# A decoder block on one core: gate and up products of the FFN summed on PSUM banks that ScalarE fills, in another order of the seven

## The chip, the core and the metric

The kernel runs on one core of one Trainium2 chip. A core has a matmul engine (TensorE; PE in the profile, PEld its weight loads), three engines for elementwise work (VectorE: DVE, ScalarE: ACT, GpSimd: POOL), a queue that mostly issues transfers (SyncE: SP), an on-chip memory (SBUF) and a small accumulator memory for matmul results (PSUM, eight banks). Each engine takes its instructions in the order of the program and waits at each for the semaphores that it names.

The metric is the device time of one execution in microseconds.

## The reference

The block normalises x (512 tokens, 2048 channels), runs two kinds of attention side by side, projects their outputs, and then runs a SwiGLU feed-forward layer with a hidden width of 5632, all in float32:

```python
def reference(x, norm1_g, w_in, ..., w_gate, w_up, w_down, final_g):
    ...
        hn = rmsnorm(h, norm1_g[l])
        proj = hn @ w_in[l]
...
        h = h + mixed @ w_out[l]

        hn2 = rmsnorm(h, norm2_g[l])
        h = h + (jax.nn.silu(hn2 @ w_gate[l]) * (hn2 @ w_up[l])) @ w_down[l]
    return rmsnorm(h, final_g)
```

Nearly all of the change lies in `hn2 @ w_gate` and `hn2 @ w_up`.

## The kernel before

**Split operands.** Every float32 operand of a large matmul is split in two: a high part (ScalarE copies it to fp32r) and a low part (VectorE subtracts the high part from the source). A product is then three matmuls: high·high, high·low and low·high (`mm`, lines 1037 to 1040, in the FFN; `mm3`, lines 167 to 169, elsewhere). The weights arrive from memory as `raw` tiles of 128 x 1024, two halves of 512 columns each. A `Job` (line 123) splits one half: `first()` runs an optional `prep`, then ScalarE writes `wh` (line 136); `second()` has VectorE write `wl` (line 139) and then runs an optional `post`. There are five slots of `wh` and five of `wl`, and four of `raw` (`LA = 4`). `next_half()` (line 174) gives PE the next split half; before that it issues the splits up to three halves ahead, the `second()` of a job one step behind its `first()`. It also issues what `later(n, f)` has put off: `f` is issued n halves after the present one, behind the splits of that step, and in the order in which it was put off. So each engine's order is written by this program order, and a waiting instruction holds all behind it on its engine.

**The FFN.** The hidden width is cut into 44 blocks f of 128. Per block, gate and up are computed together as a 2 x 2 block product by seven half-size products instead of eight (a Strassen-Winograd form). The tokens are cut into a low and a high half of 256 (`LO`, `HI`), the 2048 input channels into two halves. The four weight quarters A11, A21, A22, A12 of a block are the four `raw` tiles of that block; VectorE adds one to another in place (`comb`, line 778) to form the sums that the seven products need. Each combination is for one half of 512 columns, so there are eight per block. The activations' seven operands (B11, T1, T2, T3, T4, B21, B22) are made once, ahead of the FFN (`terms`, lines 950 to 1005).

A product (`product`, line 1025) is two halves of 12 matmuls of 128 x 256, summed in one PSUM bank. P1, P7, P4, P6 and P5 have a bank each; from block 1 on P2 goes on in the bank of P1, and P3 in the bank of P5. `after(f, name)` (line 1055) takes the results out: after P1 ScalarE copies P1 to `g` (line 1070), after P6 VectorE makes two sums with P6 and P7, after P5 two with P5 and P4, after P2 the low half of g times the factor `r2` of the second norm, after P3 the sum for g's high half (line 1087) and its product with `r2` (line 1088). Each of these is put off by one half with `later(1, ...)`. `finish` (line 1042) then does silu(g) on ScalarE (line 1045), u·g on VectorE (line 1048), its high part `ah` on ScalarE (line 1049) and its low part `al` on VectorE (line 1053), in steps that are put off by further halves, so they fall into the next block.

After every fourth block its four hidden blocks are multiplied by `w_down`: the 16 output rows of that down-projection (`down`, line 1091; a half of 24 matmuls each, weights in `rawd` tiles) are mixed into the next block's list, four behind each product from the third on. Blocks without them are called plain blocks in what follows. Block 0 has an order of its own, `ORDER0`, and forms part of its weight sums by adding transfers.

The order of the seven, and the products' jobs with their combinations, stand in `quad_jobs` (lines 770 to 823); the loads of the next block's tiles are issued by the `post` of P6, P5 and P3.

**Other places that the change touches.** `Spread` (line 232) turns four columns of factors into a row for all partitions: VectorE scales an identity matrix four times (line 239), PE multiplies it with ones. `compressed` (line 399) is the small network over compressed keys and values. The first transfers of the program are those of `sm` (all gains; line 280) and of x and the first weights, all on SP.

Of the kernel before, what the change touches and what calls it, by code (L numbers as in the profile page):

```python
# [71 lines left out]
def block_kernel(ctx: ExitStack, tc: tile.TileContext, xt, wst, wdn, smalls, wg, w2c, bias, ident_in, out):  # L72
# [25 lines left out]
    raws = {}  # L98
    state = {"dma": 0, "split": 0}
    LA = 4  # L100

    def load_to(n):
        while state["dma"] < min(n, len(units)):
            u = state["dma"]
            t = wp.tile([128, 1024], F32, tag="raw", name="raw", bufs=LA)
            for k in range(2 if u < TWO else 1):
                c = slice(512 * k, 512 * k + 512) if u < TWO else slice(0, 1024)
                sp.dma_start(t[:, c], wst[u][:, c])
            raws[u] = t
            state["dma"] += 1  # L110
            if units[u] == ("quad", 0, 1):
                pool_e.dma_start(t, wst[u + 1], accum_op=OP.add)
# [119 lines left out]
    class Spread:  # L232


        def __init__(self, col):
            self.n = col.shape[-1]
            self.r = base.tile([128, 512], F32, tag="r", name="r", bufs=2)
            for t in range(self.n):
                dve.tensor_scalar(self.r[:, 128 * t:128 * t + 128], ident, col[:, t:t + 1], None, op0=OP.mult)

        def __call__(self, copy=True, tag="misc", bufs=1):
            pb = ps.tile([128, 512], F32, tag=tag, name="prb", bufs=bufs)
# [34 lines left out]
    def tmp(name="tmp"):  # L277
        return ap_.tile([128, S], F32, tag="tmp", name=name, bufs=3)

    sp.dma_start(sm, smalls)  # L280
    xc = {}

    def load_x(k):
# [115 lines left out]
    def compressed(s):  # L399
        pt = ps.tile([128, 512], F32, tag="misc", name="phidt")  # L400
        for hb in range(2):
            for i in range(2):
                pe.matmul(pt[:, 64 * hb:64 * hb + 64], hids[:, s, 128 * hb:128 * hb + 128],
                          ident[:, 64 * i:64 * i + 64], start=(i == 0), stop=(i == 1))
        h = hidt[s]
        for hb in range(2):
            c = slice(64 * hb, 64 * hb + 64)
            if s == 0:
                act.activation(h[:, hb, 0, :], pt[:, c], AF.Silu)
            else:  # L410
                for g in range(2):
                    c = slice(64 * hb + 32 * g, 64 * hb + 32 * g + 32)
                    act.activation(h[:, hb, g, :, :], pt[:, None, c].to_broadcast([128, 3, 32]), AF.Silu)
        yield
        p2 = ps.tile([128, 512], F32, tag="misc", name="pcmp")
        if s == 0:
            for hb in range(2):
                pe.matmul(p2[:, :64], w2[:, hb, :], h[:, hb, 0, :], start=(hb == 0), stop=(hb == 1))
            dve.tensor_copy(kc, p2[:, :64])
        else:  # L420
            for g in range(2):
                for hb in range(2):
                    pe.matmul(p2[:96, 128 * g:128 * g + 128], h[:, hb, g, :, :],
                              w2[:, 2 + hb, :], start=(hb == 0), stop=(hb == 1))
                v = et_h[:, 7 + 3 * g, :]
                act.activation(v[:96], p2[:96, 128 * g:128 * g + 128], AF.Copy)
                dve.tensor_tensor(v[32:64], p2[32:64, 128 * g:128 * g + 128], v[32:64].bitcast(F32), op=OP.subtract)
# [336 lines left out]
    def load_fin(n):  # L764
        while len(fin) < min(n, KB // 2):
            k = 2 * len(fin)
            fin.append(wp.tile([128, 1024], F32, tag="raw", name="fin", bufs=LA))
            sp.dma_start(fin[-1].rearrange("p (n c) -> p n c", n=2), wdn[NPH - 1, k:k + 2].rearrange("n p c -> p n c"))

    def quad_jobs(f, order):  # L770

        u = base_u + 4 * f

        def q(i, k):
            return raws[u + i][:, 512 * k:512 * k + 512]

        def comb(o, x):
            return lambda: dve.tensor_tensor(o(), o(), x(), op=OP.add)  # L778

        def fetch(o, i, k):  # L780

            return lambda: pool_e.dma_start(o(), wst[u + i][:, 512 * k:512 * k + 512], accum_op=OP.add)

        def nxt(i):
            return lambda: load_to(u + 4 + i + 1)

        r = {}
        for k in range(2):
            A11, A21, A22, A12 = (lambda i=i, k=k: q(i, k) for i in range(4))

            if f == 0:
                r["P1", k] = Job(A11, load=None if k else nxt(-1), post=fetch(A11, 1, k))
                r["P5", k] = Job(A21, post=fetch(A21, 0, k))
                r["P7", k] = Job(A11)
                r["P2", k] = Job(A12)
                r["P4", k] = Job(A22, prep=comb(A12, A21))
                r["P6", k] = Job(A21)
                r["P3", k] = Job(A12)
            else:
                r["P1", k] = Job(A11)  # L800
                r["P7", k] = Job(A11, prep=comb(A11, A21))
                r["P4", k] = Job(A22, post=comb(A21, A22))
                r["P5", k] = Job(A21)
                r["P6", k] = Job(A22, prep=comb(A22, A11))
                r["P2", k] = Job(A12)
                r["P3", k] = Job(A12, prep=comb(A12, A22))
        if f + 1 < FB:
            if f == 0:
                r["P6", 1].post = nxt(2)
                r["P3", 1].post = nxt(3)  # L810
            else:
                r["P6", 1].post = nxt(0)
                r["P5", 1].post = nxt(1)
                r["P3", 1].post = nxt(3)
        else:
            r["P6", 1].post = lambda: load_fin(1)
            r["P5", 1].post = lambda: load_fin(2)
            r["P3", 1].post = lambda: load_fin(LA)
        r["P1", 0].even = f in (1, 2) or f % 8 == 5
        return [r[p, k] for p in order for k in range(2)]  # L820

    ORDER0 = ("P1", "P5", "P2", "P7", "P4", "P6", "P3")
    ORDER = ("P1", "P7", "P4", "P6", "P5", "P2", "P3")

    def dn_job(p, nb):
        return Job(lambda: dn[p, nb], post=load_dn)
# [123 lines left out]
    def terms(nb):  # L950
# [41 lines left out]
        def s3():  # L992
            dve.scalar_tensor_tensor(t[:, HI], k[:, LO], gk, t[:, LO], op0=OP.mult, op1=OP.add)
            low("T3", n, t[:, LO])
            high("T2", n, t[:, HI])

        def s4():
            dve.scalar_tensor_tensor(t[:, LO], h[:, LO], g, t[:, HI], op0=OP.mult, op1=OP.subtract)
            low("T2", n, t[:, HI])
            high("T4", n, t[:, LO])  # L1000

        def s5():
# [16 lines left out]
             for n, t in (("P1", "proj"), ("P7", "proj"), ("P4", "sc"), ("P6", "sc"), ("P3", "t"))}  # L1019
    banks["P5"] = ps.tile([128, 512], F32, tag="o", name="P5")  # L1020
    dbanks = {}

    st = {}

    def product(f, name):
        key = {"P2": "P1", "P3": "P5" if f else "P3"}.get(name, name)
        if key == name:
            st[key] = banks[name]
        p = st[key][:, :256]
# [1 line left out]
        for k in range(2):  # L1031
            h, l = next_half()
            for s in range(4):
                mm(p, h[:, 128 * s:128 * s + 128], l[:, 128 * s:128 * s + 128], th[:, 4 * k + s, :],
                   tl[:, 4 * k + s, :], key == name and k == 0 and s == 0, k == 1 and s == 3)

    def mm(o, wh, wl, mh, ml, start, stop):
        pe.matmul(o, wh, mh, start=start, stop=False, skip_group_check=True)  # L1038
# [16 lines left out]
    def after(f, name):  # L1055
# [10 lines left out]
        g, u = st.get("g"), st.get("u")  # L1066
        if name == "P1":
            st["g"] = ft()
            st["u"] = ft() if f else None
            act.activation(st["g"][:, LO], x("P1"), AF.Copy)  # L1070
        elif name == "P6":
            sub(g[:, HI], g[:, LO], x("P6"))
            add(u[:, LO], g[:, HI], x("P7"))
            if not f:
                dve.tensor_tensor(g[:, LO], x("P1"), st["r2"][:, LO], op=OP.mult)
                add(u[:, HI], u[:, LO], x("P5"))
                sub(u[:, LO], u[:, LO], x("P4"))
                add(g[:, HI], g[:, HI], x("P5"))
        elif name == "P5":
            add(u[:, HI], u[:, LO], x("P5"))  # L1080
            sub(u[:, LO], u[:, LO], x("P4"))
        elif name == "P2":
            dve.tensor_tensor(g[:, LO], x("P1"), st["r2"][:, LO], op=OP.mult)
            if f == FB - 1:
                finish(f, g, u, LO)
        elif name == "P3":
            add(g[:, HI], g[:, HI], x("P5" if f else "P3"))
            dve.tensor_tensor(g[:, HI], g[:, HI], st["r2"][:, HI], op=OP.mult)
            finish(f, g, u, HI if f == FB - 1 else slice(0, 512))

# [19 lines left out]
    for kind, a, b in sched:  # L1110
# [5 lines left out]
        if f == 0:  # L1116
            if name == "P7":
                r = st["rs2"] = Rsqrt(tokens(sacc), D, rab.v[:, :4])
                r.invert()
                dve.tensor_tensor(r.z, r.z, rab.y[:, :4], op=OP.mult)  # L1120
                later(1, lambda r=r: st.update(inv=Spread(r.z), r2=Spread(r.y)))
            if name == "P6":
                st["inv"] = st["inv"](False)
                act.activation(st["rs2"].rs[:, 7, :1], ones[:, :1], AF.Silu)
# [1 line left out]
                st["u"] = ft()  # L1126
            if name in ("P1", "P6", "P3"):
                later(0 if name == "P1" else 1, lambda name=name: after(0, name))
        elif name in ("P1", "P6", "P5", "P2", "P3"):
            later({(FB - 1, "P2"): 0, (FB - 1, "P3"): 3}.get((f, name), 1), lambda f=f, name=name: after(f, name))  # L1130

    def last():
# [7 lines left out]
        def scaled(r, nb, n, th):  # L1140
            h = hs[:, nb:nb + n, (LO, HI)[th]]
            o = h
            if th:
                if nb % 4 == 0:
                    st["o"] = wp.tile([128, 1024], F32, tag="raw", name="scaled", bufs=LA)
                o = st["o"].rearrange("p (a b) -> p a b", b=256)[:, nb % 4:nb % 4 + n, :]
            dve.tensor_tensor(o, h, r[:, None, :256].to_broadcast([128, n, 256]), op=OP.mult)
            sp.dma_start(out[th, :, nb:nb + n, :], o)
# [131 lines left out]
```

## Time and profile before

| | us |
|---|---|
| median of three runs | 2176.18 (2175.72 to 2179.32) |
| the profiled execution, its own time | 2175.39 |
| its span, first to last instruction | 2173.6 |
| granted PE clock, mean | 0.998 |

The profile is that of one execution. "Busy" is the time in which an engine had an instruction in work; matmuls overlap, so the mean duration of a matmul is longer than the distance from one to the next, and that distance is what a stretch costs. The same holds for VectorE and ScalarE: the next instruction can begin before the last has landed. In timelines the first two columns are the start and the duration in microseconds; a bracket at the end of a row gives the idle time of that engine ahead of the instruction and what ended it. In the list of waits the columns are the total waited, how often, and the longest; in lists of groups they are count, busy time, mean duration in ns, and idle time ahead.

The FFN begins at 836 us of the span and ends at about 2158, with the last sums and the output behind it.

### The profile page before, as it was taken

How to read it: one execution, taken by the hardware profiler on the slowest of the kernel's cores; microseconds unless marked ns; L12 is line 12 of the kernel's file. 1: busy time of each engine (PE TensorE's matmuls, PEld its weight loads, DVE VectorE, ACT ScalarE, POOL GpSimd, SP SyncE). 2: the span in 40 equal slices, each digit the busy share in tenths (PEclk: the TensorE clock that was granted, in tenths of full speed). 3: DMA queues.
4: the chain of work that ended last, by engine and by line, in shares of the span. 5: the costliest groups of instructions: out<-in, count | busy, mean ns of one | idle time of the engine just before them, and what ended most of it. 6: DMA issues, size and time to landing. Idle time of an engine off the chain costs nothing.

```text
span 2173.6 us, 39728 instructions
## 1 busy us (share of the span) xinstructions
PE 2159.9 (99%) x15776; PEld 2021.9 (93%) x15776; DVE 1566.0 (72%) x3046; ACT 965.9 (44%) x1862; POOL 42.7 (2%) x51
## 2 busy tenths in 40 slices
PE   9999999999999999999999999999999999999997
PEld 7888888888888889999999999999999999999997
DVE  6755565456667588979687777869596877878686
ACT  6544444344444255525343443435253434434356
POOL 0000000000000000000000000000000000000003
PEclk9999999999999999999999999999999999999999
DMA  6442222322224334333333333333333333333233
GB/s 224 150 135 80 90 77 70 102 80 81 80 78 164 98 97 101 115 116 100 108 105 117 97 109 106 108 96 108 117 98 107 108 117 92 114 107 108 81 124 107
DMA packets 81866, 232.28 MB, mean 107 GB/s; under 512 B 8848, under 2 KB 11536, under 8 KB 81680
## 3 DMA queue, kind: packets, MB, share of 16 engines
q1 hardware_dynamic: 80960, 228.17, 33.4%
q0 software_dynamic: 720, 1.57, 0.4%
q8 instruction: 124, 2.03, 0.4%
q14 instruction: 62, 0.51, 0.1%
HBM read 225.51 MB, written 4.19 MB: 106 GB/s over the span
## 4 chain that ended last, share of the span: by engine, by line
PE 98%; DVE 1%; ACT 0%; DMA 0%; issue 0%; SPq 0%; DVEq 0%; ACTq 0%
PE P L1040 15%; PE P L1038 15%; PE P L1039 15%; PE pp L167 7%; PE pp L169 7%; PE pp L168 7%; PE pd L1040 4%; PE pd L1039 4%; PE pd L1038 4%; PE pab L169 3%; PE pab L167 3%; PE pab L168 3%; PE pt L533 1%; PE po L168 1%; PE psc L169 1%; PE po L167 1%
## 5 line engine op out<-in xcount | busy, mean ns | idle before, releaser
L136 ACT ACTIVATE wh<-raw 128x512 fp32r<-128x512 f32 x888 | 548.7, 628 | 528.0 <-PE P L1039 208.7
L139 DVE TENSOR_TENSOR wl<-raw,wh 128x512 fp32r<-128x512 f32 x888 | 599.5, 687 | 43.9 <-ACT wh L136 42.5
L1040 PE MATMUL P<-ah,wl 128*128 128x256 f32 x1552 | 428.9, 276 | 0.2 <-DVE wl L139 0.2
L1038 PE MATMUL P<-ah,wh 128*128 128x256 f32 x1552 | 428.8, 276 | 0.0
L1039 PE MATMUL P<-al,wh 128*128 128x256 f32 x1552 | 428.8, 276 | 0.0
L1040 PEld LDWEIGHTS P<-ah,wl 128*128 128x128 f32 x1552 | 291.4, 188 | 0.4 <-DVE wl L139 0.4
L1039 PEld LDWEIGHTS P<-al,wh 128*128 128x128 f32 x1552 | 291.4, 188 | 0.0
L1038 PEld LDWEIGHTS P<-ah,wh 128*128 128x128 f32 x1552 | 291.4, 188 | 0.0
L167 PE MATMUL pp<-ah,wh 128*128 128x512 f32 x640 | 260.6, 407 | 0.0
L169 PE MATMUL pp<-ah,wl 128*128 128x512 f32 x640 | 251.1, 392 | 0.0
L168 PE MATMUL pp<-al,wh 128*128 128x512 f32 x640 | 250.3, 391 | 0.0
L778 DVE TENSOR_TENSOR raw<-raw 128x512 f32<-128x512 f32 x346 | 237.7, 687 | 3.4
L1040 PE MATMUL pd<-ah,wl 128*128 128x256 f32 x784 | 216.6, 276 | 0.0
L1039 PE MATMUL pd<-al,wh 128*128 128x256 f32 x784 | 216.5, 276 | 0.0
L1038 PE MATMUL pd<-ah,wh 128*128 128x256 f32 x784 | 216.5, 276 | 0.0
L136 ACT ACTIVATE wh<-rawd 128x512 fp32r<-128x512 f32 x160 | 101.1, 632 | 249.1 <-PE pd L1039 122.9
L1106 DVE TENSOR_TENSOR hs<-hs,pd 128x512 f32<-128x512 f32 x98 | 67.4, 688 | 122.0 <-PE pd L1040 121.7
L1038 PEld LDWEIGHTS pd<-ah,wh 128*128 128x128 f32 x784 | 147.2, 188 | 0.0
L1040 PEld LDWEIGHTS pd<-ah,wl 128*128 128x128 f32 x784 | 147.2, 188 | 0.0
L1039 PEld LDWEIGHTS pd<-al,wh 128*128 128x128 f32 x784 | 147.2, 188 | 0.0
L169 PEld LDWEIGHTS pp<-ah,wl 128*128 128x128 f32 x640 | 120.2, 188 | 28.1 <-DVE wl L139 0.4
L139 DVE TENSOR_TENSOR wl<-rawd,wh 128x512 fp32r<-128x512 f32 x160 | 110.1, 688 | 42.6 <-ACT wh L136 37.5
(275 smaller groups left out, 4560.0 us busy)
## 6 DMA issues: line engine op xcount, KB each, us to landing
raw<-in_wst_dram SPq DMA_DIRECT2D x310, 512.0 KB, 3.5
rawd<-in_wdn_dram SPq DMA_DIRECT2D x160, 256.0 KB, 2.6
bias<-in_bias_dram SPq DMA_DIRECT2D x16, 320.0 KB, 3.0
xc<-in_xt_dram SPq DMA_DIRECT2D x16, 256.0 KB, 3.0
hs<-in_xt_dram SPq DMA_DIRECT2D x16, 256.0 KB, 5.4
fin<-in_wdn_dram SPq DMA_DIRECT2D x8, 512.0 KB, 4.1
out_dram<-hs SPq DMA_DIRECT2D x8, 256.0 KB, 2.1
out_dram<-scaled SPq DMA_DIRECT2D x3, 512.0 KB, 2.8
```

Source lines behind the costliest of these rows:

```text
L136: act.activation(self.h, self.src(), AF.Copy)
L139: dve.tensor_tensor(self.l, self.src(), self.h.bitcast(F32), op=OP.subtract)
L167: pe.matmul(o, wh, mh, start=start, stop=False)
L168: pe.matmul(o, wh, ml, start=False, stop=False)
L169: pe.matmul(o, wl, mh, start=False, stop=stop)
L533: pe.transpose(p[:, 128 * (o + b):128 * (o + b) + 128], self.e[t][:, 128 * b:128 * b + 128], ident)
L778: return lambda: dve.tensor_tensor(o(), o(), x(), op=OP.add)
L1038: pe.matmul(o, wh, mh, start=start, stop=False, skip_group_check=True)
L1039: pe.matmul(o, wh, ml, start=False, stop=False, skip_group_check=True)
L1040: pe.matmul(o, wl, mh, start=False, stop=stop, skip_group_check=True)
L1106: dve.tensor_tensor(hs[:, nb, :], hs[:, nb, :], p, op=OP.add)
```

## The change

- The order of the seven products from block 1 on is P1, P4, P6, P5, P7, P2, P3 in place of P1, P7, P4, P6, P5, P2, P3.
- After P1, ScalarE copies P1's bank into P6's bank, and P6 is summed on top of that, with no start flag on its first matmul; after P6, ScalarE copies P6's bank into P7's bank, and P7 is summed on top of it. P3 goes on in the bank of P6 in place of that of P5. ScalarE also copies P4 and P5 out to `u` and `g`. VectorE's sums after P6 and P5 become two sums after P7. The operand T2 has its sign turned.
- Of the eight combinations of a block, those of P7's `prep` become P1's `post`; the others stay with their products.
- There are five slots of raw weights in place of four. The loads of the next block are issued by P6, P7 and P3.
- One of the two spreads in block 0 runs on ScalarE. The transfer of `sm` is issued by ScalarE. The last step of `compressed` runs its matmuls for both groups ahead of the copies and subtractions.

```diff
     LA = 4
+    RB = 5
...
-            t = wp.tile([128, 1024], F32, tag="raw", name="raw", bufs=LA)
+            t = wp.tile([128, 1024], F32, tag="raw", name="raw", bufs=RB)
...
-        def __init__(self, col):
+        def __init__(self, col, on_act=False):
             self.n = col.shape[-1]
             self.r = base.tile([128, 512], F32, tag="r", name="r", bufs=2)
             for t in range(self.n):
-                dve.tensor_scalar(self.r[:, 128 * t:128 * t + 128], ident, col[:, t:t + 1], None, op0=OP.mult)
+                r = self.r[:, 128 * t:128 * t + 128]
+                if on_act:
+                    act.activation(r, ident, AF.Copy, scale=col[:, t:t + 1])
+                else:
+                    dve.tensor_scalar(r, ident, col[:, t:t + 1], None, op0=OP.mult)
...
-    sp.dma_start(sm, smalls)
+    act.dma_start(sm, smalls)
...
                 for hb in range(2):
                     pe.matmul(p2[:96, 128 * g:128 * g + 128], h[:, hb, g, :, :],
                               w2[:, 2 + hb, :], start=(hb == 0), stop=(hb == 1))
+            for g in range(2):
                 v = et_h[:, 7 + 3 * g, :]
...
             else:
-                r["P1", k] = Job(A11)
-                r["P7", k] = Job(A11, prep=comb(A11, A21))
+                r["P1", k] = Job(A11, post=comb(A11, A21))
                 r["P4", k] = Job(A22, post=comb(A21, A22))
+                r["P6", k] = Job(A22, prep=comb(A22, A11))
                 r["P5", k] = Job(A21)
-                r["P6", k] = Job(A22, prep=comb(A22, A11))
+                r["P7", k] = Job(A11)
                 r["P2", k] = Job(A12)
                 r["P3", k] = Job(A12, prep=comb(A12, A22))
...
                 r["P6", 1].post = nxt(0)
-                r["P5", 1].post = nxt(1)
+                r["P7", 1].post = nxt(2)
                 r["P3", 1].post = nxt(3)
...
-    ORDER = ("P1", "P7", "P4", "P6", "P5", "P2", "P3")
+    ORDER = ("P1", "P4", "P6", "P5", "P7", "P2", "P3")
...
-            high("T2", n, t[:, HI])
+            high("T2", n, t[:, HI], -1.0)
...
-            low("T2", n, t[:, HI])
+            low("T2", n, t[:, HI], -1.0)
...
+    SEEDED = ("P6", "P7")
...
-        key = {"P2": "P1", "P3": "P5" if f else "P3"}.get(name, name)
+        key = {"P2": "P1", "P3": "P6" if f else "P3"}.get(name, name)
...
-                   tl[:, 4 * k + s, :], key == name and k == 0 and s == 0, k == 1 and s == 3)
+                   tl[:, 4 * k + s, :], not (f and name in SEEDED) and key == name and k == 0 and s == 0, k == 1 and s == 3)
...
         if name == "P1":
             st["g"] = ft()
-            st["u"] = ft() if f else None
-            act.activation(st["g"][:, LO], x("P1"), AF.Copy)
+            if f:
+                st["u"] = ft()
+                st["P6"] = banks["P6"]
+                act.activation(x("P6"), x("P1"), AF.Copy)
+            else:
+                act.activation(st["g"][:, LO], x("P1"), AF.Copy)
         elif name == "P6":
-            sub(g[:, HI], g[:, LO], x("P6"))
+            if f:
+                st["P7"] = banks["P7"]
+                act.activation(x("P7"), x("P6"), AF.Copy)
+                act.activation(u[:, LO], x("P4"), AF.Copy)
+                return
+            add(g[:, HI], g[:, LO], x("P6"))
+            dve.tensor_tensor(g[:, LO], x("P1"), st["r2"][:, LO], op=OP.mult)
             add(u[:, LO], g[:, HI], x("P7"))
-            if not f:
-                dve.tensor_tensor(g[:, LO], x("P1"), st["r2"][:, LO], op=OP.mult)
-                add(u[:, HI], u[:, LO], x("P5"))
-                sub(u[:, LO], u[:, LO], x("P4"))
-                add(g[:, HI], g[:, HI], x("P5"))
-        elif name == "P5":
             add(u[:, HI], u[:, LO], x("P5"))
             sub(u[:, LO], u[:, LO], x("P4"))
+            add(g[:, HI], g[:, HI], x("P5"))
+        elif name == "P7":
+            act.activation(g[:, HI], x("P5"), AF.Copy)
+            sub(u[:, LO], x("P7"), u[:, LO])
+            add(u[:, HI], x("P7"), g[:, HI])
...
         elif name == "P3":
-            add(g[:, HI], g[:, HI], x("P5" if f else "P3"))
+            if f:
+                add(g[:, HI], x("P6"), g[:, HI])
+            else:
+                add(g[:, HI], g[:, HI], x("P3"))
...
-                later(1, lambda r=r: st.update(inv=Spread(r.z), r2=Spread(r.y)))
+                later(1, lambda r=r: st.update(inv=Spread(r.z, True), r2=Spread(r.y)))
...
-        elif name in ("P1", "P6", "P5", "P2", "P3"):
+        elif name in ("P1", "P6", "P7", "P2", "P3"):
```

The two other tiles of the tag `raw` (`fin`, `scaled`) get five slots as well.

More of the change, by code (lines that the diff above doesn't have):

```diff
@@ L766, in load_fin @@
             k = 2 * len(fin)
-            fin.append(wp.tile([128, 1024], F32, tag="raw", name="fin", bufs=LA))
+            fin.append(wp.tile([128, 1024], F32, tag="raw", name="fin", bufs=RB))
             sp.dma_start(fin[-1].rearrange("p (n c) -> p n c", n=2), wdn[NPH - 1, k:k + 2].rearrange("n p c -> p n c"))
@@ L1144, in scaled @@
                 if nb % 4 == 0:
-                    st["o"] = wp.tile([128, 1024], F32, tag="raw", name="scaled", bufs=LA)
+                    st["o"] = wp.tile([128, 1024], F32, tag="raw", name="scaled", bufs=RB)
                 o = st["o"].rearrange("p (a b) -> p a b", b=256)[:, nb % 4:nb % 4 + n, :]
```

## The prediction

> **What bounds the kernel now.** I read the page first, then the waits of the matmul engine, then the busy time by stretches, then the timeline of one FFN block.
>
> ```profile
> span 2173.6 us, 39728 instructions
> PE 2159.9 (99%) x15776; PEld 2021.9 (93%) x15776; DVE 1566.0 (72%) x3046; ACT 965.9 (44%) x1862; POOL 42.7 (2%) x51
> ...
> PE 98%; DVE 1%; ACT 0%; DMA 0%; issue 0%; SPq 0%; DVEq 0%; ACTq 0%
> ```
> ```profile
> PE prb L245 <- DVE r L239: 1.7, 1, 1.7
> ...
> PE pcmp L423 <- DVE et_h L427: 0.7, 1, 0.7
> ...
> PE P L1038 <- DVE ft L1075: 0.3, 1, 0.3
> PE P L1040 <- DVE wl L139: 0.2, 1, 0.2
> ```
>
> PE is the bound from end to end: 98% of the chain, and only 13.7 us of the span (2173.6 − 2159.9) are not PE. The change adds and removes no matmul, so it cannot gain much; it can lose as much as it makes PE wait. In the whole FFN PE now waits twice, both in block 1 (0.3 and 0.2 us).
>
> ```profile
> 1100.00:1150.00 50.00, 50.00 (x444) 50.00 (x443) 46.77 (x83) 27.01 (x46) 0.00 (x0) 1.00 0.34 107
> 1150.00:1200.00 50.00, 50.00 (x444) 50.00 (x443) 32.84 (x55) 17.60 (x29) 0.00 (x0) 1.00 0.35 106
> ```
>
> Columns: PE, PEld, DVE, ACT, POOL, then the granted clock. PE is full in both; DVE is at 46.77 of 50 in a stretch of plain blocks (those without down-projection) and has slack only where down-projection is mixed in (32.84). So the question is whether DVE, nearly full, still delivers in time in the new order.
>
> ```profile
> 1717.57 0.28 PE L1038 MATMUL P<-B11h,wh 128*128 128x256 f32 x1
> ...
> 1717.80 0.28 PE L1040 MATMUL P<-B11h,wl 128*128 128x256 f32 x1
> ```
>
> Matmuls start every 0.113 us (0.23 for two). A weight half is 12 of them, 1.36 us; a product is two halves, 2.72 us; a block is 14 halves, 19.04 us.
>
> **The change, part by part.** *The order.* Per block f ≥ 1 it was P1 P7 P4 P6 P5 P2 P3 and becomes P1 P4 P6 P5 P7 P2 P3. The eight combinations (L778) stay, but P1 now has one behind each half, P4 too, and P6 one ahead of each: with P3 before them, four products in a row carry one per half, and P5, P7, P2 none. *The sums.* Four VectorE 256-wide operations of the old P6 and P5 steps become two at P7; ScalarE gets the seed P6←P1 (in place of its copy of P1 into g), the seed P7←P6, and copies of P4 and P5: three more. The first matmul of P6 must now wait for a ScalarE instruction that did not concern PE before. In ScalarE's order that seed stands right behind the high part `ah` of the activation of block f−1 (both fall due in P4's second half, `ah` first). `ah` waits for VectorE's product u·g (L1048), which waits its turn behind the splits and combinations. So: when does the seed end, against the start of P6?
>
> The prices, from two plain blocks of the old kernel, VectorE first:
>
> ```profile
> 1713.27 0.68 DVE L139 TENSOR_TENSOR wl<-raw,wh 128x512 fp32r<-128x512 f32 x1
> 1713.98 0.69 DVE L778 TENSOR_TENSOR raw<-raw 128x512 f32<-128x512 f32 x1
> 1714.59 0.69 DVE L139 TENSOR_TENSOR wl<-raw,wh 128x512 fp32r<-128x512 f32 x1
> ...
> 1717.77 0.42 DVE L1061 TENSOR_TENSOR ft<-ft,P 128x256 f32<-128x256 f32 x1
> 1718.23 0.42 DVE L1088 TENSOR_TENSOR ft<-ft,r 128x256 f32<-128x256 f32 x1
> 1718.57 0.69 DVE L139 TENSOR_TENSOR wl<-raw,wh 128x512 fp32r<-128x512 f32 x1
> 1719.17 1.41 DVE L778 TENSOR_TENSOR raw<-raw 128x512 f32<-128x512 f32 x2
> ...
> 1721.10 0.68 DVE L778 TENSOR_TENSOR raw<-raw 128x512 f32<-128x512 f32 x1
> 1721.70 0.69 DVE L1048 TENSOR_TENSOR ft<-ft 128x512 f32<-128x512 f32 x1
> ```
> ```profile
> 1717.70 0.63 ACT L136 ACTIVATE wh<-raw 128x512 fp32r<-128x512 f32 x1 [0.73 <-PE P L1039]
> 1718.68 0.64 ACT L1045 ACTIVATE ft<-ft 128x512 f32<-128x512 f32 x1 [0.35 <-DVE ft L1088]
> ...
> 1720.70 0.64 ACT L136 ACTIVATE wh<-raw 128x512 fp32r<-128x512 f32 x1 [0.86 <-DVE raw L778]
> 1722.42 0.64 ACT L1049 ACTIVATE ah<-ft 128x512 fp32r<-128x512 f32 x1 [1.09 <-DVE ft L1048]
> 1722.96 0.36 ACT L1070 ACTIVATE ft<-P 128x256 f32<-128x256 f32 x1
> 1723.22 1.87 ACT L136 ACTIVATE wh<-raw 128x512 fp32r<-128x512 f32 x3
> ```
>
> VectorE: a 512-wide operation holds it 0.60 us (1721.10 to 1721.70), 0.71 before one that must see its result or its reading ended (1713.27 to 1713.98; the pair of 1.41 is 0.72 + 0.69); a 256-wide 0.34 (1718.23 to 1718.57), 0.46 before one that needs it. ScalarE: a slot of weights is free 0.13 after the half that read it (1717.70 against PE's 1717.57), a split holds 0.53 and lasts 0.63, a 256-wide copy lasts 0.37; behind VectorE 0.03 (1721.70 + 0.69 to 1722.42), behind a combination 0.12 (1719.17 + 1.41 = 1720.58 to 1720.70).
>
> Already in the old order the copy of P1, at the very place that the seed takes, starts 1722.96 − 1717.57 = 5.39 us after P1's first matmul; P6 in the new order starts 4 halves = 5.44 after it. With 0.37 for the copy it would be 0.3 late without any reordering.
>
> *A plain block in the new order*, t = 0 at P2's first matmul, when P7 is done; P6 of the next block is due 8 halves later, at 10.88. ScalarE: split of P1's first half 0.13, copy of P5 0.66 to 1.03. VectorE, which needs that copy for its second sum of P7: sum 1.06; then without a pause wl 1.40, combination 2.11, wl 2.72, combination 3.43 (P1); product with r for g's low half 4.03; wl 4.37, combination 4.97, P6's first combination 5.69, wl 6.30, combination 6.90 (P4); sum with P3's bank 7.50, product with r 7.96; P6's second combination 8.30, ending at 8.98, and wl of P6's first half meanwhile; ScalarE splits P6's second half 9.09 to 9.72; wl 9.75; u·g 10.35 to 11.03; `ah` 11.06; seed 11.60 to 11.97; PE can start near 12.02 (0.05 behind its releaser, next rows). Late by 1.14 us. Behind P6's first matmul stands all of PE's queue, and behind the seed on ScalarE only the split of P5's second half, wanted 4 us later. The wait is not made up: VectorE's row starts again from P7's end, so it recurs in each block.
>
> ```profile
> 858.86 0.42 DVE L1075 TENSOR_TENSOR ft<-P,r 128x256 f32<-128x256 f32 x1
> ```
> ```profile
> 859.33 0.38 PE L1038 MATMUL P<-B11h,wh 128*128 128x256 f32 x1 [0.29 <-DVE ft L1075]
> 859.55 0.28 PE L1039 MATMUL P<-B11l,wh 128*128 128x256 f32 x1
> ...
> 867.78 0.28 PE L1039 MATMUL P<-al,wh 128*128 128x256 f32 x1
> 868.25 0.39 PE L1040 MATMUL P<-ah,wl 128*128 128x256 f32 x1 [0.19 <-DVE wl L139]
> 868.47 0.28 PE L1038 MATMUL P<-ah,wh 128*128 128x256 f32 x1
> ```
> ```profile
> 867.56 0.37 ACT L1070 ACTIVATE ft<-P 128x256 f32<-128x256 f32 x1
> ```
>
> After a wait the second matmul comes 0.22 us behind the first, not 0.113: 0.11 more per wait. So 1.25 per plain block.
>
> *Which blocks.* Blocks 2 to 43 without 5, 9, … 41 are 32: 32 × 1.25 = 40.0 us. Ahead of blocks 5, 9, … 41 (10 of them) down-projection halves give VectorE time; there it is held only by the weight slots. P4's first slot comes free at −2.72 (t from P1's start): split −2.59, wl −1.93, combinations −1.33 and −0.61, wl 0.00, combination 0.60, sum 1.20, product 1.66, combination 2.00 to 2.68, split 2.79, wl 3.45, u·g 4.05, `ah` 4.77, seed 5.31 to 5.68, PE 5.73 against 5.44: 0.29 + 0.11 = 0.4, × 10 = 4.0 us. Block 1 follows block 0's burst of sums: the old copy of P1 stands 867.56 − 859.33 = 8.23 after P1's start, the seed would end at 8.65 with 5.44 wanted: 3.2 + 0.1 = 3.3 us. Against it, the old wait for wl in block 1 falls into that longer one: 868.25 − 867.78 is 0.36 more than 0.113, and 0.11 behind it, −0.5. Together +46.8.
>
> *The seed itself* is PSUM to PSUM, which the trace lacks. The nearest pair:
>
> ```profile
> L941 ACT ACTIVATE B21h<-hs,sm 128x256 fp32r<-128x256 f32 x8 | 4.0, 496 | 0.0
> L983 ACT ACTIVATE tm<-hs,sm 128x256 f32<-128x256 f32 x8 | 3.7, 462 | 0.0
> ```
>
> Writing PSUM (tm) takes 462 ns, writing SBUF 496 from the same source. I take L1070's 0.37; the ends are 0.34 (0.034 less) and 0.46 (L983 whole): −1.5 or +3.9 us over 43 blocks. The Trainium skill, "ScalarE: Activation LUTs", section "Step-by-step: what each stage is for", says that ScalarE is nearer to PSUM and writes it faster; by that the 46.8 becomes 45.3.
>
> *The rest.* The loop over g split in two (L423) puts both pairs of matmuls ahead of the first subtraction: the 0.7 us wait goes, at most −0.7. Four of eight spreads in block 0 move to ScalarE and the product with r there (L1075) goes one place earlier: between −0.3 (that wait gone) and +0.5 (ScalarE's splits later by four spreads), taken as 0. T2's sign costs no instruction.
>
> ```profile
> 2.03 0.20 ACT L93 ACTIVATE ident<-ones 128x1 f32<-128x1 f32 x1
> ...
> 4.18 0.72 ACT L256 ACTIVATE ah<-xc,sm 128x512 fp32r<-128x512 f32 x1 [1.95 <-DMA xc<-in_xt_dram]
> ```
> ```profile
> raw<-in_wst_dram SPq DMA_DIRECT2D x310, 512.0 KB, 3.5
> ...
> sm<-in_smalls_dram SPq DMA_DIRECT2D x1, 64.0 KB, 1.9
> ```
>
> `sm` now leaves ScalarE's queue behind L93, at 2.23, lands 1.9 later at 4.1: what x gains on SP's queue, `sm` eats; ±0.3, taken as 0. Five raw slots, and loads that follow P6, P7 and P3: the tile with the shortest notice (A21 of the next block, asked for behind P7's last split, read behind P1's first) has 5 halves, 6.8 us, and lands in 3.5. Zero; with that cover gone a late tile would cost what is missing of 3.5.
>
> Sum: 46.8 − 0.7 = **+46.1 us**, on the profiled execution's own 2175.4 (span 2173.6 and 1.8 around it): 2221.5. The median shown, 2176.2, is 0.8 above that execution: 2222.
>
> **The rivals.** *VectorE keeps its lead* also in plain blocks: then every seed is late by the 0.4 of the slot limit: 42 × 0.4 + 3.3 − 0.5 − 0.7 = +18.9, 2195. For it: two 256-wide operations less per block. Against: 8 combinations in 8 halves, 1.2 us of VectorE per 1.36 before any sum.
>
> *No seed is late* (the other side): VectorE reaches u·g by 9.2 instead of 10.35, or the cast does not hold the seed. Then only the small gains stay, 0.7 and perhaps 0.5 in block 1: 2175, within what counts as no change. For it: the old order ran without a wait with more VectorE work. Against: it needs 1.1 us out of a row of operations with no pause in it. A gain of more than 4.4 us has no source among 13.7 us outside PE.
>
> *The gaps lower PE's clock.* The window rows grant 1.00 throughout, and the two old waits in block 1 (0.29 and 0.19) were too short to test it. If each gap brought one product at half speed, 43 × 2.72 = 117 us on top: 2339. The Trainium skill, "TensorE: Matmul & The Clock Gate", Part 1, has the clock halved after an idle window of about 3.4 us; by that only block 1 is near it and no other block. No row here shows it.
>
> *The change doesn't do what it says*: the banks are different ones and no matmul is added, so it does; what can fail is only when.
>
> **How the numbers follow.** Forecast 0.77, slot limit 0.09, no late seed 0.10, clock 0.02, something else slower 0.02. The forecast's own range: a chain of twenty steps may be off by 0.3 us in 32 blocks, ±10, and the seed's ends give −1.5 and +3.9: 2211 to 2232 (both at their best or worst would be rare). Downward I take in the slot limit at 2195; the no-change case and the clock stay out. 0.2% (4.4 us) is about what a measurement can tell from no change: slower 0.88, same 0.09, faster 0.03.
>
> **What would show it.** Among PE's waits a new one, P6's first matmul on ScalarE's copy into P6, some 43 times, about 1.1 us each in plain blocks and 0.3 behind down-projection, 3 us once; a plain block of 20.3 us, not 19.04; on ScalarE `ah` waiting for u·g about 1 us just ahead of the seed; DVE busy share in plain stretches lower than 46.77 of 50. Wrong it is if PE has no such wait, or the wait is P7's (its seed ends 1.03 us into P5, with 1.7 to spare), or wl ends last.

## The result, and the profile after

| | us |
|---|---|
| before, median (4 runs) | 2175.95 (2175.21 to 2179.32) |
| after, median (4 runs) | 2251.64 (2248.49 to 2253.21) |
| ratio | 1.0341 (95%: 1.0328 to 1.0353) |
| profiled execution after, its span | 2253.21, 2251.4 |

The change makes the kernel 75.7 us slower. The forecast was 46 us slower, 2222; 2251.6 lies outside its range.

The page of the changed kernel, its span, PE's busy time and the chain:

```profile
span 2251.4 us, 39710 instructions
...
PE 2214.5 (98%) x15776; PEld 2069.6 (92%) x15776; DVE 1551.8 (69%) x2956; ACT 1005.3 (45%) x1995; POOL 42.7 (2%) x51
...
PE 91%; DVE 4%; issue 2%; ACT 2%; ACTq 0%; DVEq 0%
```

PE has the same 15776 matmuls but is busy for 2214.5 us in place of 2159.9. That is already a sign that not all of the loss is waiting: PE's time outside work grew from 13.7 to 36.9 us only. Its waits in the changed kernel (total, times, longest):

```profile
PE P L1045 <- ACT P L1079: 23.8, 33, 3.3
...
PE P L1045 <- DVE ft L1089: 0.6, 1, 0.6
```

The new wait is the one forecast: P6's first matmul (L1045) on ScalarE's copy into P6's bank (L1079), 33 times. The wait for `pcmp` (0.7) is gone. Now the same stretch of both kernels, from block 1 to P3 of the last block, as windows that hold the same number of matmuls, first of the changed kernel, then of the one before (length, PE, PEld, DVE, ACT, POOL, granted clock, DMA share, GB/s):

```profile
860.00:2191.00 1331.00, 1307.12 (x11055) 1299.44 (x11055) 968.27 (x1584) 571.04 (x1021) 0.00 (x0) 1.00 0.33 100
```
```profile
860.00:2114.00 1254.00, 1253.81 (x11055) 1253.61 (x11054) 982.19 (x1671) 533.15 (x893) 0.00 (x0) 1.00 0.35 106
```

The 77 us lie here. PE idles for 23.9 us (1331.00 − 1307.12) against 0.2; the other 53 us are PE's own busy time, for the same matmuls at the same granted clock of 1.00 (some 11 of them are the matmul still in work when a wait begins, and the refill behind it). A stretch without any wait of 0.1 us or more shows where they are, two of the changed kernel and one of the old:

```profile
1450.00:1500.00 50.00, 50.00 (x443) 50.00 (x442) 30.85 (x51) 15.46 (x26) 0.00 (x0) 1.00 0.34 101
1700.00:1750.00 50.00, 50.00 (x427) 50.00 (x426) 27.85 (x45) 14.07 (x23) 0.00 (x0) 1.00 0.36 106
```
```profile
1700.00:1750.00 50.00, 50.00 (x444) 50.00 (x443) 46.46 (x82) 26.58 (x46) 0.00 (x0) 1.00 0.34 106
```

PE is full in all three, yet 427 matmuls fit in one stretch and 443 or 444 in the others: 117.1 or 112.9 ns each, and over 500 us (below) 117.7 and 113.3. There are two steady paces for the same kind of matmul. In the timeline of a plain block of the changed kernel (start, duration) the pace can be read row by row:

```profile
1405.00 0.28 PE L1047 MATMUL P<-ah,wl 128*128 128x256 f32 x1
1405.12 0.28 PE L1045 MATMUL P<-B21h,wh 128*128 128x256 f32 x1
1405.24 0.28 PE L1046 MATMUL P<-B21l,wh 128*128 128x256 f32 x1
1405.36 0.28 PE L1047 MATMUL P<-B21h,wl 128*128 128x256 f32 x1
```

I split the difference over the FFN, from its first matmul to the last of its last product, by the 11,255 distances from one start to the next. What is over 150 ns counts as a wait with its excess over 113.33; of the shorter distances the excess over 113.33 counts as pace. Waits: 35.7 us after, 1.2 before. Pace: 44.3 us after (9,954 matmuls at the 118 ns pace), 1.5 before (337). The FFN starts 0.9 earlier, and what follows its last product takes 60.4 us in place of 59.0 (1.1 of these 1.4 are pace again: 384 down-projection matmuls stand there, and they take 45.3 us in place of 44.2). Sum: 34.5 + 42.8 − 0.9 + 1.4 = 77.8, the difference of the spans. More than half of the loss is a slower pace that the prediction did not have.

When does the pace change? In the old trace it is 118 ns from the FFN's first matmul on, through most of block 0, and no wait stands ahead of it:

```profile
836.18 0.39 PE L169 MATMUL pab<-ah,wl 128*128 128x512 f32 x1
836.41 0.28 PE L1038 MATMUL P<-B11h,wh 128*128 128x256 f32 x1
836.53 0.28 PE L1039 MATMUL P<-B11l,wh 128*128 128x256 f32 x1
836.65 0.28 PE L1040 MATMUL P<-B11h,wl 128*128 128x256 f32 x1
```

It is 113 behind the first half of P1 of block 1, 118 again from the short wait for `wl` at 868 us, and 113 behind the first half of P1 of block 2. Those halves and the same ones of blocks 5, 13, 21, 29 and 37 have their weights at another place in their slot, 64 bytes further on (`even`, line 819 of the kernel before), and their own 12 matmuls take about 120 ns each. In the changed kernel most waits of P6 leave the 118 ns pace, which then lasts for whole blocks. So the theory A to test: a wait of PE puts the matmuls behind it on the 118 ns pace, and they keep it until an `even` half (called a reset below). The start of the FFN shows that a wait is not the only way into the slower pace; what starts it there was not tested. The rivals: B, summing on banks that ScalarE has written, or ScalarE's writes into PSUM, slow the matmuls; C, five slots of raw weights move the tiles in SBUF, and the new places slow them. A lower clock is out: it is 1.00 in each of the window rows.

### The profile page after: what moved, and what is told of

Its sections match the earlier page's. It is cut to its first block, busy times and chain, and to the rows that moved or that the text cites. A ratio compares the mean times of both kernels' runs of the same rounds, so it can differ in the third digit from the quotient of the medians.

```text
span 2251.4 us, 39710 instructions
## 1 busy us (share of the span) xinstructions
PE 2214.5 (98%) x15776; PEld 2069.6 (92%) x15776; DVE 1551.8 (69%) x2956; ACT 1005.3 (45%) x1995; POOL 42.7 (2%) x51
## 4 chain that ended last, share of the span: by engine, by line
PE 91%; DVE 4%; issue 2%; ACT 2%; ACTq 0%; DVEq 0%
PE P L1045 14%; PE P L1046 13%; PE P L1047 13%; PE pp L168 7%; PE pp L170 7%; PE pp L169 7%; PE pd L1045 4%; PE pd L1046 4%; PE pd L1047 4%; PE pab L168 3%; PE pab L169 3%; PE pab L170 3%; DVE wl L140 2%; PE pt L539 1%; DVE raw L784 1%
## 5 line engine op out<-in xcount | busy, mean ns | idle before, releaser
L1045 PE MATMUL P<-ah,wh 128*128 128x256 f32 x1552 | 437.9, 282 | 23.9 <-ACT P L1079 23.8
L1045 PEld LDWEIGHTS P<-ah,wh 128*128 128x128 f32 x1552 | 291.3, 188 | 31.6 <-ACT P L1079 31.3
L1045 PE MATMUL pd<-ah,wh 128*128 128x256 f32 x784 | 218.9, 279 | 0.0
L1045 PEld LDWEIGHTS pd<-ah,wh 128*128 128x128 f32 x784 | 147.3, 188 | 0.0
```

## The experiments

The times of each ratio are of the same chip; where two versions were timed on different chips, I compare their distances from the old kernel there. "Pace" and "waits" are summed as above.

**The seed one half earlier.** If the waits go, does the pace return with all the rest of the change in place?

```diff
@@ after the changed kernel, scheduling of products @@
         product(f, name)
+        if f and name == "P1":
+            later(0, lambda: act.activation(banks["P6"][:, :256], banks["P1"][:, :256], AF.Copy))
@@ after(), P1 @@
-                st["P6"] = banks["P6"]
-                act.activation(x("P6"), x("P1"), AF.Copy)
```

> The changed kernel with the seed of P6 issued one half earlier, ahead of the high part `ah` on ScalarE; all else as changed. Theory A (the cost is the wait of P6 on the late seed, plus the slower pace in which the matmuls go on after a wait, 117.8 instead of 113.3 ns from one to the next): no wait of P6 on ScalarE from block 2 on, and with no wait in them the plain blocks keep the 113.3 ns that the last half with even-placed weights leaves; 2174 to 2182 us. If the last wait ahead of the waitless part leaves the slow pace, up to 45 us more, but then a half with even-placed weights or a wait is where it changes. Rival B (matmuls that add to banks filled by ScalarE, or ScalarE's writes into PSUM, slow the matmuls themselves): waits gone, 117.8 ns in all blocks, 2176 + 44 = 2220. Rival C (five raw slots move the tiles in SBUF, and that slows the matmuls): also 2220.

2180.05 us (2178.38 to 2180.76), ratio 1.0017 (1.0008 to 1.0026). One wait of P6 is left, in block 1, and the pace is back:

```profile
PE P L1045 <- ACT P L1134: 1.3, 1, 1.3
```
```profile
1000.00:1500.00 500.00, 500.00 (x4413) 500.00 (x4412) 378.75 (x626) 225.88 (x406) 0.00 (x0) 1.00 0.32 106
```

4413 matmuls in 500 us are 113.3 ns each; the kernel before has 4412 there:

```profile
1000.00:1500.00 500.00, 500.00 (x4412) 500.00 (x4412) 387.90 (x659) 212.53 (x356) 0.00 (x0) 1.00 0.35 106
```

The seeds, the sums on filled banks, ScalarE's longer work and the five slots are all still there, so none of them slows the matmuls: B falls, and C with it. The place of one copy among ScalarE's instructions costs 72 us (75.7 − 3.8). Of the 3.8 us that are left, 1.8 are waits and 2.0 pace: a short wait in block 4 (0.34 us from start to start at a down-projection half) leaves 118 ns from 932 us to the `even` half of block 5.

**Five slots alone**, the kernel before with `bufs=5` for the three tiles of the tag `raw`.

> The kernel before, with five slots of raw weights in place of four and nothing else of the change. Theory A: no new wait, the pace stays 113.3 ns, 2176 us within 4. Rival C (the moved tiles slow the matmuls): 117.8 ns throughout, 2176 + 44 = 2220.

2176.33 us (2175.55 to 2180.2), ratio 1.0002 (0.9993 to 1.0011). No cost: the 0 of the prediction. The profiled execution was the one at 2180.2; it has no more waits than the old kernel, but here the `even` half of block 2 did not change the pace, and 118 ns lasted to block 5, two windows of it:

```profile
900.00:980.00 80.00, 80.00 (x682) 80.00 (x681) 62.19 (x104) 28.44 (x48) 0.00 (x0) 1.00 0.33 106
985.00:1035.00 50.00, 50.00 (x443) 50.00 (x443) 46.65 (x82) 26.45 (x46) 0.00 (x0) 1.00 0.31 107
```

682 matmuls in 80 us before block 5's `even` half, and 443 in 50 behind it. The pace term of this execution is 5.4 us, 3.9 above the old kernel's 1.5: about the distance from the other runs. That suggests that the old kernel's scatter (2175.2 to 2179.3) is one of pace as well; the last run below bears on it.

**A wait without the change**: the old kernel, and one copy that P6 has to wait for.

```diff
         f, name = a, b
+        if f and name == "P6":
+            act.activation(banks["P6"][:, :256], banks["P4"][:, :256], AF.Copy)
         product(f, name)
```

> The kernel before, its order, sums and four slots unchanged, with one copy of P4's bank into P6's bank on ScalarE ahead of P6 in each block from 1 on; P6 starts with its start flag, so nothing is summed on the copy. P4 stands right ahead of P6 here, so P6 has to wait for the copy. Theory A: 43 waits of about 0.7 us idle, 0.9 from start to start, 0.8 us lost each = 34 us, and most blocks at 117.8 ns after them, up to 48 us: 2245 to 2260, with none of the change's seeds, sums or slots. Rival B (summing on seeded banks): only the waits, 2176 + 34 = 2210. Rival C: 2210 too.

2248.57 us (2247.73 to 2248.74), ratio 1.0332 (1.0316 to 1.0347): 72.3 us more than the old kernel, where the changed kernel has 75.7, with none of the change.

```profile
PE P L1038 <- ACT P L1116: 16.1, 33, 1.5
```

33 waits and not 43 (behind P4 of every fourth block stand down-projection halves that cover the copy). In a plain block the start-to-start distance at the wait is 0.73 us and the next one 0.22, against 0.113 twice: 0.73 lost. Of 73.2 us more of span, 24.7 are waits and 45.8 pace. All but one of the 33 waits are followed by 118 ns (the one in block 1 is not).

**One wait**: the same copy in block 3 alone (`if (f, name) == (3, "P6")`), and `even` cut to `f in (1, 2)`.

> The kernel before with that copy in block 3 alone, and with the even-placed weight halves of blocks 5, 13, 21, 29 and 37 taken out (blocks 1 and 2 keep theirs). Theory A: one wait of about 0.8 us, and the slow pace from there to the end, some 10,400 matmuls x 4.45 ns = 46 us: 2222 us from a single wait. If the pace is not kept between waits, or a wait has nothing to do with it: 2177 us.

2224.37 us (2224.1 to 2224.91), ratio 1.0221 (1.0204 to 1.0238). The wait and the pace on both sides of it:

```profile
906.69 0.28 PE L1039 MATMUL P<-T4l,wh 128*128 128x256 f32 x1
906.80 0.28 PE L1040 MATMUL P<-T4h,wl 128*128 128x256 f32 x1
907.54 0.39 PE L1038 MATMUL P<-ah,wh 128*128 128x256 f32 x1 [0.46 <-ACT P L1116]
907.77 0.28 PE L1039 MATMUL P<-al,wh 128*128 128x256 f32 x1
907.88 0.28 PE L1040 MATMUL P<-ah,wl 128*128 128x256 f32 x1
908.00 0.28 PE L1038 MATMUL P<-ah,wh 128*128 128x256 f32 x1
908.12 0.28 PE L1039 MATMUL P<-al,wh 128*128 128x256 f32 x1
```
```profile
1000.00:1500.00 500.00, 500.00 (x4248) 500.00 (x4247) 373.04 (x629) 202.47 (x339) 0.00 (x0) 1.00 0.32 103
1500.00:2000.00 500.00, 500.00 (x4247) 500.00 (x4247) 372.55 (x629) 203.04 (x339) 0.00 (x0) 1.00 0.32 102
```

A single idle time of 0.46 us, with no `even` half behind it, costs 48 us: the distance from start to start goes from 0.11 ahead of it (113 ns since the half of block 2) to 0.12 behind it, and stays at 117.7 ns (500 / 4248) for the 1,250 us that follow, with PE full. The share of busy time shows nothing of it; the number of matmuls in a window does. Nor does it take a copy of ScalarE into PSUM: the wait at 868 us in the old trace was for VectorE's `wl`.

**No reset, and no new wait**: the old kernel without the line that sets `even`.

> The kernel before with no even-placed half in the FFN (it has them in blocks 1, 2, 5, 13, 21, 29, 37). No wait is added. Theory A: block 0 and the two short waits of block 1 leave the slow pace, nothing resets it: some 11,000 matmuls x 4.45 ns = 49 us, 2225 us. If the pace depended on the order or on ScalarE's load: 2176.

2224.91 us (2224.21 to 2225.18), ratio 1.022 (1.0206 to 1.0234). Waits 1.0 us, pace 49.7: the pace is 118 ns from the FFN's first matmul on, as in the old kernel, and without an `even` half nothing ends it. This run shows what the resets are worth; it doesn't show what a wait does.

```profile
1000.00:1500.00 500.00, 500.00 (x4247) 500.00 (x4247) 372.69 (x630) 202.87 (x338) 0.00 (x0) 1.00 0.35 103
```

**The hold with a reset behind each wait**: the old kernel with the copies in each block, and P6's second half `even`.

```diff
         r["P1", 0].even = f in (1, 2) or f % 8 == 5
+        r["P6", 1].even = f > 0
```

> The kernel before with the hold in each block (33 waits) and P6's second half at the even place. Theory A: the waits stay at 26 us, the slow pace is gone but for a half or two per block (about 5 us): 2204 to 2210, against 2248.6 without the even place. If the pace hangs on the copy and not on the wait's restart: 2248 to 2252.

2205.33 us (2204.88 to 2205.53), ratio 1.013 (1.0116 to 1.0144): 43 us less than without that line. The waits are the same (16.1 us of idle time; over the whole FFN 25.9 lost, as there); the pace term is 5.9 us in place of 47.3.

```profile
PE P L1039 <- ACT P L1117: 16.1, 33, 1.5
```

**The changed kernel with that same line.** Here the prediction's own sum can be seen, since it assumed the 113 ns pace.

> The changed kernel, with the weights of P6's second half put at the even place in their slot in each block from 1 on, so that the half right behind the wait resets the pace. Nothing else differs. Theory A: waits of P6 as the prediction had them (due earlier at 113.3 ns, so about 1.3 us lost in each of 32 plain blocks against 0.88 now), pace 113.3 ns between them: 2176 + 42 to 47 of waits + 3 to 5 of the even halves themselves and the slow halves ahead of them = 2222 to 2228, against 2251.6. If the even place doesn't reset the pace: 2252 to 2255.

2229.84 us (2228.3 to 2231.78), ratio 1.0243 (1.0229 to 1.0257), 1.8 above the expected range. Waits 50.3 us, pace 6.2: the waits are 49.1 more than in the old kernel, above the 42 to 47 expected, and the pace 4.7 more, within its 3 to 5.

```profile
PE P L1046 <- ACT P L1080: 37.0, 38, 3.3
```
```profile
1386.37 0.39 PE L1046 MATMUL P<-ah,wh 128*128 128x256 f32 x1 [1.03 <-ACT P L1080]
...
1406.83 0.38 PE L1046 MATMUL P<-ah,wh 128*128 128x256 f32 x1 [1.03 <-ACT P L1080]
```

The waits are longer than in the changed kernel (1.03 idle, 1.30 lost, against 0.60 and 0.88): the earlier PE asks, the longer it waits for the same seed. The end of the `even` half is where the pace changes, from 0.12 to 0.113:

```profile
1409.41 0.28 PE L1046 MATMUL P<-ah,wh 128*128 128x256 f32 x1
1409.53 0.28 PE L1047 MATMUL P<-al,wh 128*128 128x256 f32 x1
1409.65 0.28 PE L1048 MATMUL P<-ah,wl 128*128 128x256 f32 x1
1409.77 0.28 PE L1046 MATMUL P<-T1h,wh 128*128 128x256 f32 x1
...
1410.23 0.28 PE L1047 MATMUL P<-T1l,wh 128*128 128x256 f32 x1
1410.34 0.28 PE L1048 MATMUL P<-T1h,wl 128*128 128x256 f32 x1
1410.45 0.28 PE L1046 MATMUL P<-T1h,wh 128*128 128x256 f32 x1
```

**The parts outside the products**: the old kernel with the spread on ScalarE, `sm` on ScalarE's queue, and the split loop, as in the diff above.

> The kernel before, with only the parts of the change that lie outside the products: one spread of block 0 on ScalarE, the transfer of the gains issued by ScalarE, and the loop over both groups in the small network split. All theories: 0 to 1.5 us less than before, 2174.8 to 2176.3; the FFN starts 0.9 earlier, as in the changed kernel, and nothing behind it differs. If the changed kernel's spread on ScalarE delays block 0: up to 1 us more instead.

2178.28 us (2174.13 to 2179.4), ratio 1.0003 (0.9994 to 1.0012). The profiled execution has a span of 2173.0 us, 0.6 below the old kernel's, and its FFN starts at 835.8 in place of 836.4. But the 11 runs fall in two groups, four at 2174.1 to 2174.7 and seven at 2178.2 to 2179.4, so the median says nothing of a gain of this size, and lies outside what was expected.

**The same with a second reset**, block 3 added: `f in (1, 2, 3) or f % 8 == 5`.

> The kernel before with the parts outside the products (as in the run with those alone) and one more even-placed half, in block 3. The runs of those parts alone fall in two groups, near 2174.4 and near 2178.6; a profile of the five-slot kernel at 2180.2 shows the slow pace from 868 to 985, where the even half of block 2 had not reset it. Theory A: a second reset one block later leaves at most 20 us of slow pace (0.8 us), so one group: 2174 to 2175.5, 1 to 1.5 below before. If the two groups have another cause: still two groups, median 2176 to 2179.

2175.51 us (2174.04 to 2176.13), ratio 0.9984 (0.9975 to 0.9993). The upper group is gone. In the profile the half of block 2 fails here too, and that of block 3 brings the 113 ns pace, at 900 us. The old kernel's own runs beside it were mostly in its upper group (median 2179.71, 2175.36 to 2180.64), so the ratio shows what a reset that holds is worth, not a faster kernel: the five old runs of the lower group have a median of 2176.09, and 0.6 us from that is not told from scatter. The run keeps none of the change to the products.

## Why the prediction was wrong

**PE is the bound, and a gain has no source.** Right: no run with the products changed is faster than before.

**The chain to the late seed.** Right, to 0.06 us. The plain block with P2's first matmul at 1405.12 (rows above) ends in these rows of the changed kernel's timeline:

```profile
1412.65 0.41 DVE L1068 TENSOR_TENSOR ft<-P,ft 128x256 f32<-128x256 f32 x1
1413.10 0.42 DVE L1107 TENSOR_TENSOR ft<-ft,r 128x256 f32<-128x256 f32 x1
...
1414.90 0.69 DVE L140 TENSOR_TENSOR wl<-raw,wh 128x512 fp32r<-128x512 f32 x1 [0.18 <-ACT wh L137]
1415.51 0.69 DVE L1055 TENSOR_TENSOR ft<-ft 128x512 f32<-128x512 f32 x1
...
1416.23 0.63 ACT L1056 ACTIVATE ah<-ft 128x512 fp32r<-128x512 f32 x1 [0.84 <-DVE ft L1055]
...
1416.77 0.37 ACT L1079 ACTIVATE P<-P 128x256 f32<-128x256 f32 x1
...
1417.19 0.38 PE L1045 MATMUL P<-ah,wh 128*128 128x256 f32 x1 [0.60 <-ACT P L1079]
1417.41 0.28 PE L1046 MATMUL P<-al,wh 128*128 128x256 f32 x1
```

With t = 0 at 1405.12: sum with P3's bank 7.53 (7.50 in the prediction), product with r 7.98 (7.96), wl 9.78 (9.75), u·g 10.39 (10.35), `ah` 11.11 (11.06), seed 11.65 (11.60), P6 12.07 (12.02). The early seed shows the cause as well: with the copy ahead of `ah` the wait is gone. The refill of 0.11 behind a wait is there too (0.22 to the second matmul).

**The failed step: "Matmuls start every 0.113 us".** The prediction took this distance from the old trace as a property of the matmul and kept it for the new kernel. It depends on what went before: 0.113 holds since the last `even` half that worked, and most waits end it. This adds 42.8 us, and 1.1 behind the last product: 44 of the 78 us between the two profiled executions. The term of pace stood at nothing in the sum. The old trace had the sign of it, in the rows right behind those that the prediction quoted for the refill:

```profile
868.59 0.28 PE L1039 MATMUL P<-al,wh 128*128 128x256 f32 x1
868.71 0.28 PE L1040 MATMUL P<-ah,wl 128*128 128x256 f32 x1
...
868.94 0.28 PE L1039 MATMUL P<-al,wh 128*128 128x256 f32 x1
```

They start 0.12 apart, and went unread; so did the purpose of a flag that moves 12 matmuls' weights in seven blocks. The rival that came nearest, "The gaps lower PE's clock", had the right form (a cost behind the gap that is not the gap) and the wrong mechanism: the granted clock stays 1.00, and the price is 4 ns per matmul for as long as nothing resets it, not half speed for one product.

**1.25 per plain block × 32 = 40.0.** At the 113 ns pace 1.30 (1.305 − 0.113 at the wait, 0.222 − 0.113 behind it): 41.6, as the changed kernel with resets shows. In the changed kernel itself 0.87 to 0.88 in 28 of the 32, and 1.30 to 1.31 in the three that PE reached at 113 ns: at 118 ns P6 comes due at 8 × 12 × 117.7 ns = 11.30 in place of 10.88, so 0.43 of the lateness disappears in the slower pace. A plain block is 20.66 us from P6 to P6 in the trace (20.3 forecast):

```profile
1396.53 0.39 PE L1045 MATMUL P<-ah,wh 128*128 128x256 f32 x1 [0.60 <-ACT P L1079]
...
1437.85 0.39 PE L1045 MATMUL P<-ah,wh 128*128 128x256 f32 x1 [0.61 <-ACT P L1079]
```

That is two blocks, 41.32.

**0.4 in each of ten blocks behind down-projection.** 0.40 with resets on average; in the changed kernel 0.09 to 0.26 in nine of them, again because of the pace, and 0.37 in block 21, ahead of which PE had been at 113 ns since block 20. **Block 1, 3.3**: 3.6 (3.59 from start to start and 0.23 behind it).

**The sum itself.** Waits forecast 46.8; 49.1 more than before with the resets, 34.5 in the changed kernel. So the forecast of 2222 describes the kernel with resets (2229.8, of which 4.7 are the resets' imperfect pace) and not the one that was run.

**The seed's copy, 0.37 (0.34 to 0.46).** Right. The groups of the changed kernel for the copy within PSUM (L1079) and one of the same size from PSUM to SBUF (L1095), with count, busy time and mean ns:

```profile
L1079 ACT ACTIVATE P<-P 128x256 f32<-128x256 f32 x43 | 15.7, 366 | 0.0
L1095 ACT ACTIVATE ft<-P 128x256 f32<-128x256 f32 x43 | 15.7, 366 | 0.0
```

The Trainium skill, "ScalarE: Activation LUTs", section "Step-by-step: what each stage is for", has ScalarE write PSUM faster than SBUF. Here, reading PSUM, there is no difference of 1 ns, so the measurement decides. The prediction's pair, 462 and 496, read SBUF and differed in the type written as well (f32 and fp32r), so it didn't show what the place alone does.

**Five slots, and the rest.** Five slots cost nothing (2176.33). The parts outside the products bring the FFN forward by 0.6 alone and 0.9 in the changed kernel (it starts at 835.5 to 835.8 in the five profiles with them, at 836.3 to 837.5 in the six without); 0.7 was forecast. The second seed, P7's, was never waited for, as forecast.

## What to carry to other kernels

A matmul's distance to the next, read from a trace, can be a state of the stream and not a constant: before a change that makes PE wait is costed, count the matmuls per window behind the waits that the old trace already has, and multiply any excess by all matmuls up to what resets it. PE's busy share and its granted clock don't show such a loss; matmuls per microsecond do. A producer that PE waits for belongs ahead of long chains on its engine's queue: moving one 0.37 us copy half a product forward gave back 72 us.

## What the runs showed of the hardware that was not expected

- The same 128x256 matmuls, each with a weight load of its own, run at 113.3 or at 117.7 ns from one to the next with PE full and a granted clock of 1.00 (4412 and 4247 in 500 us). One pace is kept for over 1,200 us. The Trainium skill, "TensorE: Matmul & The Clock Gate", Part 2, section "Back-to-back issue gap", gives one distance for an isolated warm matmul, columns / 2.4 + 2.5, by which an estimate for 256 is 109.2 ns; for streams with a weight load to each matmul it has figures for 128 and 512 columns only. Neither pace here is 109.2, and the section names no two paces for the same matmul.
- Idle times of 0.2 to 3.3 us nearly always leave the slower pace (32 of 33 in the held old kernel); in the changed kernel four left the faster. It is also there from the FFN's first matmul, with no wait.
- Twelve matmuls whose weights lie at the other place of the slot, 64 bytes on, bring the faster pace back, mostly but not always: all 76 did that stand behind a wait of P6 (33 in the held old kernel, 43 in the changed one), but in the profiled run with five slots the half of block 2 did not, nor in the last run, nor did those of blocks 2 and 5 in the changed kernel. Where it works, the twelve distances settle at 120 ns; in the four that failed they go on between 117 and 124. Why the place does this, and why it sometimes fails, stays open; no run here separates the weight loads from the reading of the moving operand.
